# A decoder trunk's last product of values, written as pairs of matmuls of 64 contraction rows

## Chip, cores and metric

The kernel runs on one core of one Trainium2 chip. The metric is the device time of one execution in microseconds (us), the median of several runs. The profile is of one execution; its times count from the first instruction it recorded.

## The reference

Two layers over 256 tokens of width 2048, all in float32. Layer 0 is a Mamba-2 mixer. After it, one product makes the keys and values that the second layer's attention shares. Cut to what matters here:

```python
x = _layer_norm(alpha * x + (1 + gate) * y, ln_g[0], ln_b[0])   # end of layer 0
k, v = jnp.split(x @ kv_w, 2, axis=-1)     # each (256, 3 groups x 8 heads x 128)
...
h = x * (1.0 + scale) + shift              # layer 1 works on h
q, z = jnp.split(h @ b_in_w[0], [3072], axis=-1)
# three head groups of windowed attention over k and v, merged, gated by silu(z)
y = o @ b_out_w[0]
```

## The kernel before

Float32 accuracy is made of three products in the one-pass float32 type F32R: every operand is split into a high part (a rounded copy) and a low part (the rest), and high x high, high x low and low x high are summed in PSUM. Weights stream from HBM in pieces of 128 x 1024: SyncE loads one into `raw` (L118), ScalarE copies it to `whi` (L126), VectorE subtracts for `wlo` (L127).

Contraction runs over 2048 = 16 blocks of 128 rows, `kt`. The activations after layer 0 lie with channels on partitions, in `xhi` and `xlo`: per `kt` a tile of 128 channels x 256 tokens (in the profile they are called `act`).

The values are six products of 512 columns, each by `tm_chunk` (L226): for each of 8 pieces, 2 blocks `kt`, 2 token blocks `b` of 128 and 3 terms, with 128 x 128 activations as the stationary operand and 128 x 512 weights as the moving one: 96 matmuls, on L217, L218 and L219. The two sums, of 128 tokens x 512 columns each, fill one PSUM bank each (`acc`, of the pool `mm` with four banks). `values_out` (L905) then copies each bank to `vt` on ScalarE (L907). The first two products are computed ahead in one loop (L936 to L940), then come the keys (`cm_join`), then the other four products of values (L945).

After them the activations are scaled and shifted in place for layer 1 (L950 to L954), which needs each block `kt` read by all key and value products first. Then `queries` starts (matmuls of L176 and L178), whose products go to other banks of `mm`.

The order on each engine is not that of the source. `arrange` (L1637) takes all recorded instructions with what each depends on, and plans them with a list scheduler. Each instruction has a price (`price`, L1147): for a matmul, how long it holds the engine and how long until its result is there. After eight rounds of planning forward and backward, random changes of the keys are tried, up to 260 rounds in all, and the plan with the earliest end is kept. Matmuls into the same bank keep the order in which they were written; others may be placed in any order that their operands allow. The plan fixes each engine's program; PE runs that program.

Of the kernel before, what the change touches and what calls it, by code (L numbers as in the profile page):

```python
# [11 lines left out]
F32 = mybir.dt.float32  # L12
F32R = mybir.dt.float32r
I32 = mybir.dt.int32
AF = mybir.ActivationFunctionType
ALU = mybir.AluOpType
AX = mybir.AxisListType
PSUM = bass.MemoryType.PSUM
DRAM = bass.MemoryType.DRAM

P = 128
L = 256
D = 2048
KT = D // P
# [47 lines left out]
def trunk(ctx, tc, xT, x, ada0, par, cst, bias, lnrow, ada, wdt, win, wsub, wout, wkv, wk, wbin, wbout, out):  # L72
    nc = tc.nc
    del PINS[:]
    V, S, T = nc.vector, nc.scalar, nc.tensor
# [131 lines left out]
    def tm_piece(src, q, ps, ahi, alo, k0=0, k1=KT, raw=None, n=1):  # L207

        tm_mults(q, split(load_piece(src[q]) if raw is None else raw, n=n), ps, ahi, alo, k0, k1, range(2))
# [13 lines left out]
    def tm_pair():  # L223
        return [mm.tile([P, 512], F32, name="acc") for _ in range(2)]

    def tm_chunk(src, ahi, alo, nk=KT, rate=(0, 1), k0=0, pre=None, keep=()):  # L226

        ps = tm_pair()
        n = nk // 2 - len(keep)
        for q in range(k0 // 2, n):  # L230
            if pre:
                pre(q)
            tm_piece(src, q, ps, ahi, alo, k0, nk)
            background(*rate)
        held = [(q, split(load_piece(src[q]), into=into)) for q, into in zip(range(n, nk // 2), keep)]
        for b in range(2):
            for q, w in held:
                tm_mults(q, w, ps, ahi, alo, k0, nk, (b,))
        return ps
# [29 lines left out]
    def shift(i, kt):  # L269
        return mod[i][:, kt, 0:1]  # L270
# [69 lines left out]
    def drain():  # L340
        while jobs:
            jobs.pop(0)()
# [8 lines left out]
    with ExitStack() as cA:  # L351
# [14 lines left out]
        with ExitStack() as cS:  # L366
# [38 lines left out]
            def product(kind, g, pre=None):  # L405
# [4 lines left out]
                if kind == "z":  # L410
                    ps = tm_chunk(src, hh_, hl_, rate=R, k0=k0, pre=pre)
                    if g not in sz:
# [7 lines left out]
                for w in range(2):  # L420
                    ps = cm_wide(wsub[2 * WSUB.index((kind, g)) + w], hp, hhi, rate=R, k0=k0)
                    for n in range(2):
# [13 lines left out]
            with ExitStack() as c0:  # L436
# [70 lines left out]
                rest = flat[1][:, :512].rearrange("p (j n) -> p j n", j=2)  # L507
# [105 lines left out]
                f, half, low, dots = noted["first"], noted["half"], noted["low"], noted[("dot", 1)]  # L613
# [10 lines left out]
                high, hhis = noted["high"], noted["hhi"]  # L624
# [7 lines left out]
            px = pe = cS.enter_context(tc.tile_pool(name="px", bufs=2, reuse_waits="tile"))  # L632
            R = (1, 5)

# [203 lines left out]
        for n in range(4):  # L838
            ps = tm_chunk(wout[n], lambda kt: yhi[kt // 16][:, kt % 16, :], lambda kt: ylo[kt // 4][:, kt % 4, :],
                          nk=2 * KT, rate=(1, 3) if n else (0, 1), pre=None if n else y_ahead,  # L840
                          keep=[[pa.tile([P, 1024], F32R, name=f"y{2 * i + j}") for j in range(2)] for i in range(HELD)] if n == 3 else ())
# [13 lines left out]
        xp, xhi, xlo = high_low()  # L855
# [41 lines left out]

    with ExitStack() as cL:
        pl = cL.enter_context(tc.tile_pool(name="pl", bufs=3, reuse_waits="tile"))
        R = (2, 5)  # L900
        blocks = [(wk[6 * hq + 2 * g + w], kk[hq][:, g, 2 * w:2 * w + 2, :])
                  for hq in range(2) for g in range(NG) for w in range(2)]
        values = [(wkv[2 * g + hq], vt[hq][:, g]) for hq in range(2) for g in range(NG)]

        def values_out(ps, dst):  # L905
            for b in range(2):
                S.activation(dst[:, b, :], ps[b], AF.Copy)  # L907

        def open_block(b):

            if b:
                open_tiles(b, pl, "xtmp")
            for ps in pss:
                ps.append(mm.tile([P, 512], F32, name="acc"))
            for q in range(NOPEN // 2):
                if b == 0:
                    ws.append([split(load_piece(src[q])) for src, _ in values[:2]])
                for ps, (hi, lo) in zip(pss, ws[q]):
                    for k in range(4):
                        low, k = k // 2, k % 2  # L920
                        h_, l_ = (t[:, 2 * q + k, b * P:b * P + P] for t in (xhi, xlo))
                        if low:
                            T.matmul(ps[b], l_, hi[:, k, :], start=False, stop=False)
                            continue
                        T.matmul(ps[b], h_, hi[:, k, :], start=q == k == 0, stop=False)
                        T.matmul(ps[b], h_, lo[:, k, :], start=False, stop=False)

        pss, ws = [[], []], []
        for b in range(2):
            open_block(b)  # L930
        for c0_ in range(P * NOPEN, D, 512):
            for b in range(2):
                normal(b, c0_, c0_ + 512, b == 0)
        for q in range(NOPEN // 2, KT // 2):
            for i in range(NOPEN if q == NOPEN // 2 else 2 * q + 4, min(2 * q + 6, KT)):
                x_tiles(i, pl, "xtmp")  # L936
            for ps, (src, _) in zip(pss, values):
                tm_piece(src, q, ps, hx, lx)
        for ps, (_, dst) in zip(pss, values):
            values_out(ps, dst)  # L940
        queue(pl, cols1[16:])
        jobs.append(lambda: gate_out(1))
        for src, dst in blocks:
            cm_join(src, dst, rate=R)
        for src, dst in values[2:]:  # L945
            values_out(tm_chunk(src, hx, lx, rate=R), dst)
        drain()

        ada_bias(1, slice(0, KT), slice(0, 2))
        for kt in range(KT):  # L950
            t = pl.tile([P, L], F32, name="htmp")
            S.activation(t, xhi[:, kt, :].bitcast(F32), AF.Identity, bias=shift(1, kt), scale=scale(1, kt))
            V.scalar_tensor_tensor(t, xlo[:, kt, :].bitcast(F32), scale(1, kt), t, op0=ALU.mult, op1=ALU.add)
            split_act(xhi[:, kt, :], xlo[:, kt, :], t)  # L954

        for n in range(4):
            cs_ = slice(512 * n, 512 * n + 512)
            lnr = [pl.tile([P, 512], F32, name=f"lnr{i}", bufs=2) for i in range(2)]
            for i in range(2):
                bcast(lnr[i], lnrow, i * D + 512 * n)  # L960
            for b in range(2):
                V.tensor_tensor(u[b][:, cs_], u[b][:, cs_], lnr[0], op=ALU.mult)
                V.tensor_tensor(u[b][:, cs_], u[b][:, cs_], lnr[1], op=ALU.add)
# [6 lines left out]
    dmat, amask = bs[:, CD:CD + NKEY], bs[:, CA:CA + NKEY]  # L970
    R = (0, 1)

# [82 lines left out]
    for n in range(2):  # L1055
        ps = tm_chunk(wbout[n], *og, nk=H)
# [18 lines left out]
    ps = [tm_pair() for _ in range(2)]  # L1075
# [15 lines left out]
    for i, w in enumerate((slice(0, 256), slice(256, 512))):  # L1091
        c = slice(1536 + w.start, 1536 + w.stop)
        half = (mm.tile([P, 512], F32, name="acc") if i else ps[1][1])[:, :w.stop - w.start]
        for q in range(4):
            hi, lo = held[4 + q]
# [6 lines left out]
    for po_, c in chunks[-1:] + chunks[:-1]:  # L1102
        k, c = c.start // 512, slice(c.start % 512, c.start % 512 + c.stop - c.start)
# [13 lines left out]
    r, mean = ln_scale((1,), st8, False)  # L1117
# [29 lines left out]
def price(x, e):  # L1147

    outs, ins = _aps(x.outs), _aps(x.ins)
    o = outs[0]  # L1150
    if e == "SP":
        return 0.36, 3.0 if str(o.bass_ap.tensor.space) == "DRAM" and hasattr(o.bass_ap.tensor, "tag") else 0.0, None, _n(o) * list(o.ap)[0][1] * 4
    if e == "PE":
        n = _n(ins[0])
        if "float32r" in str(ins[0].dtype):
            return (n / 2400 + 0.0133 if n < 512 else 0.2268), 0.177 + n / 2400, None, 0
        if x.is_transpose:
            return 0.109, 0.273, None, 0
        if list(ins[0].ap)[0][1] == 1:
            return 1.3, 1.5, None, 0  # L1160
        c = max(0.1105, n * 2 / 2400 + 0.0025)
        return 2 * c, c + 0.165 + n * 2 / 2400, None, 0
    n = max(_n(a) for a in ins + [o])
    ps = any(str(a.bass_ap.tensor.space) == "PSUM" for a in ins + [o])
    ptr = sum(_n(a) == 1 for a in ins[1:]) if n > 2 else 0
    if e == "Activation":
        f = str(x.func).split(".")[1]
        d = (0.165 + n / 1190 if ps else 0.19 + n / 1175) + 0.085 * ptr
        return d - 0.095, d, {"Silu": 1, "Exp": 2, "Sqrt": 3}.get(f), 0
    if e == "DVE":  # L1170
        k = type(x).__name__
        if k == "InstReciprocal" and n > 8:
            d = 0.15 + n / 160
        elif k == "InstTensorScalarPtr" and not x.is_scalar_tensor_tensor and not ps:
            d = 0.15 + n / 1850 + 0.05 * (n > 64) + 0.05 * ptr
        else:
            d = 0.152 + n / 960 + 0.057 * ptr
        return d - 0.083 + 0.08 * (len(outs) > 1), d + 0.08 * (len(outs) > 1), None, 0
    return 0.2 + n / 400, 0.2 + n / 370, None, 0
# [572 lines left out]
```

## Time and profile before

| | |
|---|---|
| median of 3 runs | 1241.44 us (1239.98 to 1241.45) |
| the profiled execution: span from first to last instruction | 1238.4 us |
| median above the span | 3.0 us |
| TensorE (PE) busy | 1227.6 us, 99% |
| VectorE (DVE) busy | 1035.9 us, 84% |
| ScalarE (ACT) busy | 703.1 us, 57% |
| HBM traffic | 269 GB/s over the span |

The page has no time of its own for the profiled execution besides the span, so the 3.0 us stand for what lies around it. Busy times are unions of the instructions' durations. PE's matmuls overlap in the array: each lasts longer than the time after which the next one starts, so the spacing of starts is the rate and the duration is not. "PEld" are the loads of the stationary operand. A row of a timeline gives start, duration, engine, line, operation, output and inputs, then the part of the array that the weights fill ("128*16" is 128 rows and 16 columns) and the shape of the moving operand.

### The profile page before, as it was taken

To read this page: it belongs to the slowest core of one execution; us is meant where nothing else is said; L and a number is where in the kernel's file an instruction comes from. 1 tells how busy PE (TensorE), PEld (TensorE's weight loads), DVE (VectorE), ACT (ScalarE), POOL (GpSimd) and SP (SyncE) were. 2 spreads that over 40 slices of the span, in tenths; PEclk is the share of its full clock that TensorE was granted. 3 is DMA by queue.
4 is the path that set the end of the run, shared out by engine and by line. 5 is a ranking of instruction groups with operands and counts; after the bars stand their busy time and mean duration, and the time that the engine had idled before them with its cause. 6 is when DMAs were issued, how large, how long until landed. Compare 5 with 4: busy or idle time off the path is not lost.

```text
span 1238.4 us, 18082 instructions
## 1 busy us (share of the span) xinstructions
PE 1227.6 (99%) x6712; PEld 1058.1 (85%) x6712; DVE 1035.9 (84%) x1481; ACT 703.1 (57%) x1054; POOL 0.2 (0%) x4
## 2 busy tenths in 40 slices
PE   8999999999999999999999999999999999999998
PEld 8889888888888888888888888888888888888886
DVE  6999998989999999978888699998865746757677
ACT  4655466768948589864335455444446644444561
POOL 0000000000000000000000000000000000000000
PEclk9999999999999999999999999999999999999999
DMA  9999977656696855748998669999985563551671
GB/s 368 422 422 421 422 271 241 223 189 234 263 339 224 318 182 190 245 154 294 384 386 308 233 221 369 412 377 378 353 308 187 200 192 103 168 182 64 203 285 68
DMA packets 81743, 334.47 MB, mean 270 GB/s; under 512 B 9108, under 2 KB 9844, under 8 KB 69496
## 3 DMA queue, kind: packets, MB, share of 16 engines
q1 hardware_dynamic: 81656, 333.33, 73.8%
q8 instruction: 52, 0.85, 0.3%
q14 instruction: 35, 0.29, 0.1%
HBM read 331.11 MB, written 2.18 MB: 269 GB/s over the span
## 4 chain that ended last, share of the span: by engine, by line
PE 86%; DMA 11%; DVE 2%; ACT 1%; issue 0%; SPq 0%; ACTq 0%
PE acc L176 27%; PE acc L178 14%; PE acc L217 12%; PE acc L218 12%; PE acc L219 12%; DMA raw<-in_win 8%; DMA araw<-in_ada 2%; PE py L729 2%; PE aux L993 1%; PE aux L699 1%; PE po L1017 1%; PE po L1006 1%; PE aux L994 1%; PE aux L721 1%; DMA y<-in_ada 1%; PE aux L783 0%
## 5 line engine op out<-in xcount | busy, mean ns | idle before, releaser
L126 ACT ACTIVATE whi<-raw 128x1024 fp32r<-128x1024 f32 (+1 forms) x393 | 409.7, 1049 | 342.2 <-PE acc L176 131.6
L127 DVE TENSOR_TENSOR wlo<-raw,whi 128x1024 fp32r<-128x1024 f32 (+1 forms) x393 | 471.2, 1211 | 119.2 <-ACT whi L126 113.3
L176 PE MATMUL acc<-act,whi 128*128 128x512 f32 x1456 | 376.8, 395 | 0.0
L176 PEld LDWEIGHTS acc<-act,whi 128*128 128x128 f32 x1456 | 262.5, 188 | 45.7
L218 PE MATMUL acc<-wlo,act 128*128 128x512 f32 x672 | 257.0, 393 | 0.2 <-DVE wlo L127 0.2
L217 PE MATMUL acc<-whi,act 128*128 128x512 f32 x672 | 249.4, 395 | 1.3 <-ACT whi L126 0.7
L299 DVE SCALAR_TENSOR_TENSOR araw<-araw,cb__72 128x2048 f32<-128x2048 f32 x92 | 210.3, 2285 | 7.0 <-DMA araw<-in_ada 6.7
L178 PE MATMUL acc<-act,wlo 128*128 128x256 f32 x1456 | 212.1, 284 | 0.0
L178 PEld LDWEIGHTS acc<-act,wlo 128*128 128x128 f32 x1456 | 200.4, 190 | 13.5 <-issue 0.5
L219 PE MATMUL acc<-whi,act 128*128 128x512 f32 x432 | 163.0, 392 | 0.0
L218 PEld LDWEIGHTS acc<-wlo,act 128*128 128x128 f32 x672 | 126.0, 188 | 27.1 <-DVE wlo L127 1.1
L217 PEld LDWEIGHTS acc<-whi,act 128*128 128x128 f32 x672 | 125.3, 188 | 27.8 <-ACT whi L126 1.2
L219 PEld LDWEIGHTS acc<-whi,act 128*128 128x128 f32 x432 | 81.1, 188 | 16.7 <-issue 0.7
L219 PE MATMUL acc<-whi,ylo 128*128 128x512 f32 x240 | 89.8, 392 | 0.0
L219 PEld LDWEIGHTS acc<-whi,ylo 128*128 128x128 f32 x240 | 45.0, 188 | 9.3 <-DVE ylo L789 0.2
L164 PE MATMUL acc<-act,whi 128*128 128x256 f32 x208 | 51.6, 284 | 0.8 <-ACT whi L126 0.4
L165 PE MATMUL acc<-act,wlo 128*128 128x256 f32 x208 | 51.9, 284 | 0.0
L162 PE MATMUL acc<-act,whi 128*128 128x256 f32 x208 | 42.0, 284 | 0.0
L164 PEld LDWEIGHTS acc<-act,whi 128*128 128x128 f32 x208 | 38.0, 191 | 2.4 <-ACT whi L126 0.6
L687 ACT ACTIVATE seg<-cbc,cumT 128x128 f32<-128x128 f32 x128 | 39.8, 389 | 0.0
L165 PEld LDWEIGHTS acc<-act,wlo 128*128 128x128 f32 x208 | 38.1, 191 | 0.8
L384 DVE SCALAR_TENSOR_TENSOR cacc<-ct,prm,cacc 128x255 f32<-128x255 f32 (+2 forms) x84 | 36.2, 477 | 1.0 <-ACT cacc L381 0.9
(269 smaller groups left out, 1147.1 us busy)
## 6 DMA issues: line engine op xcount, KB each, us to landing
araw<-in_ada SPq DMA_DIRECT2D x92, 1024.0 KB, 7.3
raw<-in_win SPq DMA_DIRECT2D x86, 512.0 KB, 9.8
raw<-in_wsub SPq DMA_DIRECT2D x70, 512.0 KB, 4.4
raw<-in_wout SPq DMA_DIRECT2D x64, 512.0 KB, 5.2
raw<-in_wbin SPq DMA_DIRECT2D x64, 512.0 KB, 3.4
raw<-in_wkv SPq DMA_DIRECT2D x48, 512.0 KB, 4.7
raw<-in_wk SPq DMA_DIRECT2D x48, 512.0 KB, 6.7
cbc<-cumd SPq DMA_DIRECT2D x16, 512.0 KB, 5.0
```

Source lines behind the costliest of these rows:

```text
L126: a = S.activation(hi[:, c_], raw[:, c_], AF.Copy)
L127: m = V.tensor_tensor(lo[:, c_], raw[:, c_], hi[:, c_].bitcast(F32), op=ALU.subtract)
L162: T.matmul(o, hi[:, k, c_], alo[:, kt, :], start=False, stop=kt == k1 - 1, skip_group_check=True)
L164: note("product", T.matmul(o, hi[:, k, c_], ahi[:, kt, :], start=kt == k0 and n % 2 == 0, stop=False, skip_group_check=True))
L165: T.matmul(o, lo[:, k, c_], ahi[:, kt, :], start=False, stop=False, skip_group_check=True)
L176: T.matmul(ps[n], hi[:, k, c_], both[:, kt], start=first, stop=False, skip_group_check=True)
L178: T.matmul(ps[n][:, 0, :], lo[:, k, c_], high[:, kt, :], start=first, stop=False, skip_group_check=True)
L217: begin = T.matmul(ps[b], h_, hi[:, k, :], start=kt == k0, stop=False)
L218: T.matmul(ps[b], h_, lo[:, k, :], start=False, stop=False)
L219: end = T.matmul(ps[b], l_, hi[:, k, :], start=False, stop=kt == k1 - 1)
L299: V.scalar_tensor_tensor(raw, raw, 1.0, cb_, op0=ALU.mult, op1=ALU.mult, accum_out=to)
L687: m = S.activation(seg[:, hh, b, :], cbc[:, hh, b, :], AF.Relu, bias=cumT[:, b, h0 + hh:h0 + hh + 1], scale=-1.0)
```

## The change

The sixth and last product of values is no longer made by `tm_chunk`. A new `rows_chunk` writes each of its 96 matmuls as two: one with the channels in partitions 0 to 63, called `low` in the source, and one with those in partitions 64 to 127, called `high`. (By partition number, `low` is the lower half, and so it is called below.) Each works on 64 contraction rows and all 512 columns. The two sum into banks of their own, `low` in two banks of `mm` (`acc` in the profile) and `high` in two banks of a new pool `rest`. At the end ScalarE copies each `high` bank to `vt` and VectorE adds the `low` bank to it.

The price of an F32R matmul with fewer than 128 contraction rows is new as well: it holds the engine for 0.1134, where a full one of 512 columns has 0.2268, and its result is there after 0.39, as for the full one. The whole program is planned anew with it, and the order of instructions differs in all stages.

```diff
+        rest = cL.enter_context(tc.tile_pool(name="rest", bufs=2, space=PSUM))
...
+        def rows_chunk(src, dst, rate):
+            low, high = tm_pair(), [rest.tile([P, 512], F32, name="rest") for _ in range(2)]
+            for q in range(KT // 2):
+                hi, lo = split(load_piece(src[q]))
+                for k in range(2):
+                    kt = 2 * q + k
+                    for b in range(2):
+                        h_, l_ = (t[:, kt, b * P:b * P + P] for t in (xhi, xlo))
+                        for i, (x_, w_) in enumerate(((h_, hi), (h_, lo), (l_, hi))):
+                            for ps, r in ((low, slice(0, 64)), (high, slice(64, P))):
+                                T.matmul(ps[b], x_[r], w_[r, k, :], start=kt == i == 0, stop=kt == KT - 1 and i == 2)
+                background(*rate)
+            for b in range(2):
+                S.activation(dst[:, b, :], high[b], AF.Copy)
+                V.tensor_tensor(dst[:, b, :], low[b], dst[:, b, :], op=ALU.add)
...
-        for src, dst in values[2:]:
+        for src, dst in values[2:5]:
             values_out(tm_chunk(src, hx, lx, rate=R), dst)
+        for src, dst in values[5:]:
+            rows_chunk(src, dst, R)
...
         if "float32r" in str(ins[0].dtype):
+            if list(ins[0].ap)[0][1] < P:
+                return 0.1134, 0.39, None, 0
             return (n / 2400 + 0.0133 if n < 512 else 0.2268), 0.177 + n / 2400, None, 0
```

In the changed kernel the new matmuls are line 921.

## The prediction, as it was put on record

> **What bounds the kernel now.** I read the page first: its head, the busy times and the 40 slices.
>
> ```profile
> span 1238.4 us, 18082 instructions
> PE 1227.6 (99%) x6712; PEld 1058.1 (85%) x6712; DVE 1035.9 (84%) x1481; ACT 703.1 (57%) x1054; POOL 0.2 (0%) x4
> PEclk9999999999999999999999999999999999999999
> PE 86%; DMA 11%; DVE 2%; ACT 1%; issue 0%; SPq 0%; ACTq 0%
> ```
>
> TensorE (PE) is busy all the time, at full granted clock, and makes up 86% of the chain that ended last. The table of windows shows whether this holds at the place of the change.
>
> ```profile
> 900.00:1000.00 100.00, 100.00 (x485) 84.39 (x485) 65.36 (x84) 55.29 (x78) 0.00 (x0) 1.00 0.66 224
> 946.00:972.00 26.00, 26.00 (x122) 21.62 (x122) 22.52 (x39) 22.68 (x41) 0.00 (x0) 1.00 0.57 196
> ```
>
> The columns are the window, its length, then busy time (and instructions) of PE, PEld, DVE, ACT and POOL, the clock, the DMA share and GB/s. The window from 946 to 972 us is that of the last product of values: the timeline of ScalarE has the copies of the product before it at 946.25 and 949.34, and its own at its end.
>
> ```profile
> 946.25 0.60 ACT L907 ACTIVATE vt<-acc 128x512 f32<-128x512 f32 x1 [0.53 <-PE acc L219]
> ...
> 970.49 0.57 ACT L907 ACTIVATE vt<-acc 128x512 f32<-128x512 f32 x1
> ...
> 972.52 0.59 ACT L907 ACTIVATE vt<-acc 128x512 f32<-128x512 f32 x1
> ```
>
> PE has no idle time there, so a microsecond of PE's stream put in or taken out in this stage moves the end by a microsecond, as long as what feeds it keeps up. How long one matmul holds PE is read from starts, not from its duration, which includes the way through the array. Timeline of PE:
>
> ```profile
> 947.19 0.39 PE L217 MATMUL acc<-whi,act 128*128 128x512 f32 x1
> ...
> 952.86 0.39 PE L217 MATMUL acc<-whi,act 128*128 128x512 f32 x1
> ```
>
> Between these two rows' starts lie 25 matmuls of 512 columns: 5.67/25 = 0.2268 us each. The product has 16 blocks of contraction rows, 2 blocks of tokens and 3 terms, so 96 matmuls, 96 x 0.2268 = 21.8 us.
>
> **What a half matmul costs.** The change makes 192 matmuls of these 96, each with 64 contraction rows and still 512 moving columns. No trace row has one of 64 rows, so I bound it. These groups say what a duration follows:
>
> ```profile
> L176 PE MATMUL acc<-act,whi 128*128 128x512 f32 x1456 | 376.8, 395 | 0.0
> L178 PE MATMUL acc<-act,wlo 128*128 128x256 f32 x1456 | 212.1, 284 | 0.0
> L783 PE MATMUL aux<-cc,y 128*128 128x128 f32 x64 | 10.2, 272 | 0.0
> ...
> L323 PE MATMUL aux<-cc,mod x2: 270/270/270, 446.2 to 956.5; 128*16 128x128 f32 x2
> ```
>
> With half the moving columns the mean falls from 395 to 284 ns. Filling less of the array does not help: L323, which loads 16 of the 128 columns (its row gives least, median and greatest), takes 270 ns, and L783, which loads all, 272. So a matmul's own time follows its moving columns, which the change keeps, and a half matmul alone should hold its half for 0.2268 us. The two halves can share a slot of 0.2268 us (0.1134 each, which the planner's new price says), or each takes its own (0.2268 each). Those are the two ends: 21.8 us for the product as before, or 192 x 0.2268 = 43.5 us, 21.8 more.
>
> Which of them holds depends on the order, and here the change does something that its text does not show. The source writes the lower and the upper half of a pair next to each other, but the planner places each matmul for itself. On PE, in the middle of the product, where acc_8905 and acc_8906 are the two token blocks' banks, the kernel before has:
>
> ```order
> L217 MATMUL acc_8905<-whi_8928,act0_6760 128x512
> L218 MATMUL acc_8905<-wlo_8929,act0_6760 128x512
> L219 MATMUL acc_8905<-whi_8928,act0_6760 128x512
> L217 MATMUL acc_8906<-whi_8928,act0_6760 128x512
> L218 MATMUL acc_8906<-wlo_8929,act0_6760 128x512
> L219 MATMUL acc_8906<-whi_8928,act0_6760 128x512
> ```
>
> The changed one has there, with acc_8908 and acc_8909 for the lower half and rest_8910 and rest_8911 for the upper:
>
> ```order
> L921 MATMUL acc_8908<-whi_8945,act0_6760 128x512
> L921 MATMUL acc_8908<-wlo_8946,act0_6760 128x512
> L921 MATMUL acc_8908<-whi_8945,act0_6760 128x512 x2
> L921 MATMUL acc_8908<-wlo_8946,act0_6760 128x512
> L921 MATMUL acc_8908<-whi_8945,act0_6760 128x512
> L921 MATMUL acc_8908<-whi_8975,act0_6760 128x512
> L921 MATMUL rest_8910<-whi_8945,act0_6760 128x512
> L921 MATMUL rest_8910<-wlo_8946,act0_6760 128x512
> L921 MATMUL rest_8910<-whi_8945,act0_6760 128x512
> L921 MATMUL acc_8909<-whi_8945,act0_6760 128x512
> ```
>
> Seven of the lower half stand in a row, then three of the upper, then the lower again: the pairs are torn apart. Two matmuls for the same half cannot share a slot. At the end of the product the kernel before has:
>
> ```order
> L217 MATMUL acc_8906<-whi_9042,act1_6761 128x512
> L218 MATMUL acc_8906<-wlo_9043,act1_6761 128x512
> L219 MATMUL acc_8906<-whi_9042,act1_6761 128x512
> L176 MATMUL acc_9183<-act0_6760,whi_9186 128x512
> L218 MATMUL acc_8905<-wlo_9043,act1_6761 128x512
> L219 MATMUL acc_8905<-whi_9042,act1_6761 128x512
> ```
>
> And the changed one:
>
> ```order
> L921 MATMUL acc_8908<-whi_9131,act1_6761 128x512 x2
> L921 MATMUL acc_8908<-wlo_9132,act1_6761 128x512
> L921 MATMUL acc_8908<-whi_9131,act1_6761 128x512
> L921 MATMUL acc_8909<-whi_9131,act1_6761 128x512 x2
> L921 MATMUL acc_8909<-wlo_9132,act1_6761 128x512
> L921 MATMUL acc_8909<-whi_9131,act1_6761 128x512
> L921 MATMUL rest_8911<-whi_9131,act1_6761 128x512
> L921 MATMUL rest_8911<-wlo_9132,act1_6761 128x512
> L921 MATMUL rest_8911<-whi_9131,act1_6761 128x512
> L176 MATMUL acc_9286<-act0_6760,whi_9290 128x512 x4
> ```
>
> Eight of the lower half, three of the upper, then the queries' first full matmuls. Does PE take later ones early? The trace of the kernel before, at that end:
>
> ```profile
> 967.96 0.39 PE L217 MATMUL acc<-whi,act 128*128 128x512 f32 x1
> 968.18 0.39 PE L218 MATMUL acc<-wlo,act 128*128 128x512 f32 x1
> 968.41 0.39 PE L219 MATMUL acc<-whi,act 128*128 128x512 f32 x1
> 968.64 0.39 PE L176 MATMUL acc<-act,whi 128*128 128x512 f32 x1
> 968.86 0.39 PE L218 MATMUL acc<-wlo,act 128*128 128x512 f32 x1
> ```
>
> It is the program's order to the last matmul, though L176 and L218 go to different banks. [...]
>
> So I count with three rules: order is kept; a half matmul holds its half for 0.2268 us; it may start with the one ahead of it if that is of the other half and shares its slot with no other. Over the whole product the 192 stand in 59 unbroken runs of one half, up to 11 long, with 54 direct changes of half (9 full matmuls, 8 of them of the product before, stand between the others). Going through the list, 45 times two share a slot, which leaves 192 - 45 = 147 slots, where 96 were before: 51 x 0.2268 = 11.6 us more.
>
> **The other terms.** Switching between full and half matmuls happens 10 times. The nearest row is the transpose that loads 16 columns amid full matmuls:
>
> ```profile
> 517.28 1.04 PE L783 MATMUL aux<-cc,y 128*128 128x128 f32 x8
> ...
> 956.26 0.39 PE L219 MATMUL acc<-whi,act 128*128 128x512 f32 x1
> 956.48 0.27 PE L323 MATMUL aux<-cc,mod 128*16 128x128 f32 x1
> 956.51 0.48 PE L217 MATMUL acc<-whi,act 128*128 128x512 f32 x1
> 956.82 0.39 PE L218 MATMUL acc<-wlo,act 128*128 128x512 f32 x1
> ```
>
> From 956.26 to 956.82 are 0.56 us; two full matmuls take 0.454 of it and a transpose (1.04 - 0.27)/7 = 0.11, as in L783. Nothing is left for a drain; I take 0. [...] This row shows none for columns. A drain here could be no more than the way through the array, 0.39 - 0.2268 = 0.16 us, so 1.6 us for ten; that is the upper end. A slot could also end 0.0125 us sooner where two share it, or last 0.013 longer if two weight loads need it; the chain in order of time has both prices:
>
> ```profile
> 976.62 1.68 PE acc L178 x14
> 978.31 3.64 PE acc L176 x16
> ```
>
> A matmul of 256 columns, with its own weight load, takes 0.120 us and one of 512 takes 0.2275: twice 0.120 less 0.2275 is 0.0125 of fixed cost, and two loads fit in 0.240. Over 45 shared slots either is 0.6 us; I take 0. The evacuation gains two additions on VectorE, each like
>
> ```profile
> L730 DVE TENSOR_TENSOR y<-py,y 128x512 f32<-128x512 f32 x16 | 10.9, 683 | 0.1
> ```
>
> so 1.4 us, in a window where DVE is busy 22.5 of 26 us and which grows by 11.6; the values are wanted only by the second half of the heads, much later: 0. Without that cover it would be 1.4. ScalarE still makes two copies. Loads and splits are as many as before, ahead of a slower PE: 0. The scale and shift of the activations (L952), written in place, follow the last reader block by block as before: 0. The planner's search gave a new order for all of the kernel; PE idles 1238.4 - 1227.6 = 10.8 us in all, most of it at the start and the end, and no row says that the new order waits more or less: 0, with 2 us either way.
>
> The sum is +11.6 us on the profiled execution, 1238.4 to 1250.0 of span; the median of the runs shown, 1241.44, lies 3.0 above the span, so 1253.0. About 0.2% (2.5 us) is what a measurement can tell here.
>
> **Rivals.** First, PE keeps two streams, so that pairs overlap however they stand: all 192 fit in 96 slots, for 1241.4, or 1240.2 if the fixed 0.0125 is hidden 96 times. It decides if one half can run ahead of the other by a run of up to 11 matmuls. This is the way to no loss at all. [...] The trace speaks against it with its kept order of starts. I give it 0.12. Second, no overlap at all: 192 slots, 21.8 us more, 1263.2, and up to 1264.8 with the drains. No row shows two matmuls at one time, which is for it, and nothing in this kernel has been shown to share the array; 0.24. Third, the new order elsewhere happens to save or avoid PE's idle time beside the first rival; this alone makes it faster, by 3 us or more: 0.04. The forecast has 0.60.
>
> **How the numbers follow.** The forecast's own range is 1253.0 less 0.6 and 2, plus 0.6, 1.6 and 2: 1250 to 1257. The second rival's is 1261 to 1267. A range from 1249 to 1266 takes in the forecast and nearly all of the second rival, 0.8 together; the first and third lie below it. Faster: 0.04. Same: 0.10, of the first rival; its remaining 0.02 goes to slower, with the forecast and the second rival, 0.86.
>
> **What would show it.** In the changed profile, the product's window should be 11.6 us longer and PE still busy throughout; starts in a run of one half 0.227 us apart; at a change of half, two starts close together; at the switches nothing. Starts 0.227 apart at changes of half too would show the second rival; starts 0.113 apart inside runs the first. The argument is wrong if runs of one half go faster than 0.2268 per matmul, or if the stage grows and the end does not move.

## The result, and the profile after

The changed kernel takes 1247.45 us (median; 1246.21 to 1247.82), the kernel before, in four runs, 1241.0: a ratio of 1.0052, 95% interval 1.0037 to 1.0066. It is slower, as forecast, but by 6.45 us and not by 11.6. The forecast of 1253.0 and the range from 1249 both miss it.

Lines of the page of the changed kernel that answer to those of before:

```profile
span 1246.0 us, 18268 instructions
PE 1233.8 (99%) x6808; PEld 1063.3 (85%) x6808; DVE 1038.9 (83%) x1483; ACT 707.4 (57%) x1056; POOL 0.2 (0%) x4
```

PE is as full as before: 96 matmuls and 96 weight loads more. The profiled execution itself took 1247.82 us, 1.8 above its span. (The spans of the two profiles differ by 7.6 us; each is of one execution, so the medians count for the difference.) The window of the product and the groups of its matmuls:

```profile
946.00:977.00 31.00, 31.00 (x212) 25.49 (x211) 20.16 (x33) 21.24 (x36) 0.00 (x0) 1.00 0.45 144
```

```profile
L921 PE MATMUL rest<-whi,act 64*128 64x512 f32 x64 | 21.1, 400 | 0.0
L921 PE MATMUL acc<-wlo,act 64*128 64x512 f32 x32 | 12.3, 399 | 0.0
```

A half matmul lasts as long as a full one (400 against 395 ns on average), as predicted from the moving columns. The surprise is in the starts. First, the timeline of PE in the first full stretch of halves:

```profile
951.43 0.49 PE L921 MATMUL rest<-whi,act 64*128 64x512 f32 x1
951.44 0.49 PE L921 MATMUL acc<-whi,act 64*128 64x512 f32 x1
951.77 0.39 PE L921 MATMUL rest<-whi,act 64*128 64x512 f32 x1
951.77 0.39 PE L921 MATMUL acc<-wlo,act 64*128 64x512 f32 x1
952.00 0.39 PE L921 MATMUL acc<-whi,act 64*128 64x512 f32 x1
952.00 0.39 PE L921 MATMUL rest<-whi,act 64*128 64x512 f32 x1
952.23 0.39 PE L921 MATMUL acc<-wlo,act 64*128 64x512 f32 x1
952.24 0.39 PE L921 MATMUL rest<-wlo,act 64*128 64x512 f32 x1
```

In PE's program the same matmuls stand next to each other in this order (numbered here from 1; `rest` is the upper half):

```
1 rest whi
2 acc whi     3 acc wlo     4 acc whi     5 acc wlo
6 rest whi
7 acc whi
8 rest whi    9 rest wlo
```

The upper half's second matmul, number 6, starts at 951.77, together with number 3 and ahead of 4 and 5. So PE does not keep the program's order between the halves: each half runs its own in order, 0.227 us apart and never less than 0.224, and here a matmul started while up to three earlier ones of the other half had not. Matching all 192 starts to the program, each half's in its order (the names of the weights, `whi` or `wlo`, then agree for every one), the number of earlier matmuls still to come is 0, 1, 2 or 3 and never more: 18 times it is three.

The same timeline where the lower half stands eleven times in a row:

```profile
956.60 0.39 PE L921 MATMUL rest<-whi,act 64*128 64x512 f32 x1
956.68 0.39 PE L921 MATMUL acc<-wlo,act 64*128 64x512 f32 x1
956.90 0.84 PE L921 MATMUL acc<-whi,act 64*128 64x512 f32 x3
...
958.26 0.39 PE L921 MATMUL acc<-whi,act 64*128 64x512 f32 x1
958.27 0.49 PE L921 MATMUL rest<-whi,act 64*128 64x512 f32 x1
958.49 0.39 PE L921 MATMUL acc<-whi,act 64*128 64x512 f32 x1
```

From 956.83, 0.227 us after its matmul of 956.60, until 958.27 the upper half has nothing to do: its next matmul stands behind the run, and starts when three of the run are still to come. Here a run costs time. And at the first change from full matmuls to halves and back:

```profile
947.16 0.39 PE L218 MATMUL acc<-wlo,act 128*128 128x512 f32 x1
947.48 0.49 PE L921 MATMUL rest<-whi,act 64*128 64x512 f32 x1
947.49 0.49 PE L921 MATMUL acc<-whi,act 64*128 64x512 f32 x1
947.91 0.50 PE L219 MATMUL acc<-whi,act 128*128 128x512 f32 x1
948.24 0.40 PE L217 MATMUL acc<-whi,act 128*128 128x512 f32 x1
948.48 0.39 PE L219 MATMUL acc<-whi,act 128*128 128x512 f32 x1
```

From 947.16 to 948.48 are 1.32 us for three full matmuls and a pair, which at 0.2268 each is 0.91: one visit to the halves costs 0.41. The pair itself starts within 0.01 us.

The stretch of the product, with the 8 full matmuls and the transpose inside it, runs from 947.48 to 976.10 (the last start is at 975.87), 28.6 us. The same work in the kernel before, 104 x 0.2268 + 0.11, is 23.7. So 4.9 of the 6.45 us are lost in the product. To split them I worked the list of starts through by three rules: a half's matmuls 0.2268 apart, at most three overtaken, and the step prices just seen (0.095 more into the halves, 0.194 out, 0.11 for a first step after an idle time). The rules give 28.5 us, and the starts deviate from the measured ones by 0.09 us on average. Without changing prices it is 26.2, with an unlimited reach besides 24.6. So, roughly, taking the terms off one after the other: 0.9 us for halves that stand alone between full matmuls, 1.6 for runs beyond the reach, 2.3 for changing and restarting.

### The profile page after: what moved, and what is told of

Same layout as the page of the kernel before. It is cut to its first block, busy times and chain, and to the rows that moved or that the text cites. A ratio compares the mean times of both kernels' runs of the same rounds, so it can differ in the third digit from the quotient of the medians.

```text
span 1246.0 us, 18268 instructions
## 1 busy us (share of the span) xinstructions
PE 1233.8 (99%) x6808; PEld 1063.3 (85%) x6808; DVE 1038.9 (83%) x1483; ACT 707.4 (57%) x1056; POOL 0.2 (0%) x4
## 4 chain that ended last, share of the span: by engine, by line
PE 81%; DMA 11%; DVE 4%; ACT 3%; issue 1%; SPq 0%; DVEq 0%; ACTq 0%
PE acc L176 26%; PE acc L178 13%; PE acc L217 10%; PE acc L218 10%; PE acc L219 10%; DMA raw<-in_win 9%; DMA araw<-in_ada 2%; PE py L729 2%; DVE wlo L127 1%; ACT whi L126 1%; PE acc L921 1%; PE rest L921 1%; DVE araw L299 1%; PE aux L1013 1%; PE po L1037 1%
## 5 line engine op out<-in xcount | busy, mean ns | idle before, releaser
L218 PE MATMUL acc<-wlo,act 128*128 128x512 f32 x640 | 245.1, 394 | 0.4 <-DVE wlo L127 0.4
L217 PE MATMUL acc<-whi,act 128*128 128x512 f32 x640 | 237.9, 394 | 1.5 <-ACT whi L126 0.6
L219 PE MATMUL acc<-whi,act 128*128 128x512 f32 x400 | 150.0, 392 | 0.0
L217 PEld LDWEIGHTS acc<-whi,act 128*128 128x128 f32 x640 | 119.8, 188 | 26.4 <-ACT whi L126 0.8
L218 PEld LDWEIGHTS acc<-wlo,act 128*128 128x128 f32 x640 | 120.0, 188 | 25.8 <-DVE wlo L127 1.0
L219 PEld LDWEIGHTS acc<-whi,act 128*128 128x128 f32 x400 | 75.1, 188 | 16.0 <-issue 1.1
```

Of the source, the lines that this page charges most:

```text
L217: begin = T.matmul(ps[b], h_, hi[:, k, :], start=kt == k0, stop=False)
L219: end = T.matmul(ps[b], l_, hi[:, k, :], start=False, stop=kt == k1 - 1)
```

## The experiments

Theory W is this reading: two streams with a reach of three, and a price for changing between full and half matmuls. Rival I is the prediction's (order kept, only neighbours overlap), rival H says that a pair simply costs more, whatever its order. To hold everything else fixed, the first five kernels start from the plan of the kernel before, and the first four keep it instruction for instruction: the planner sees each pair as one full matmul, and the second half and the two additions are put in afterwards. ScalarE copies the lower bank there and VectorE adds the upper one. Times of the kernel before are 1240.84 us in each comparison below.

**Pairs kept together.** The edit, on the plan's way into the program:

```diff
+            if x.name in pair:
+                h, q = pair[x.name]
...
+                out.append((e, x))
+                held.append(h)
+                if len(held) == RUN:
+                    put()
```

`x` is a lower half, at the place of its full matmul, `h` its upper half, and `put` writes the held ones; `RUN` is 1 here, 3 and 12 in the next two.

> The order of the kernel before is kept, instruction for instruction; only each matmul of the last product of values becomes two of 64 rows, the second right behind the first, and the two additions are put in behind the copies. Theory W (the halves are two streams, of which one may start a matmul ahead of at most three earlier ones that have not started; a visit from full matmuls to halves and back costs 0.4 us; the rest of the loss came from the new order elsewhere): all pairs overlap, six visits cost 2.6 us, so 1243.6 us. Rival H (a pair costs more whatever its order, 0.278 us for 0.227, since the product took 4.9 us more): 1245.9. Rival I (order kept, only neighbours overlap): the same pairs overlap here, 1241.0 to 1243.6.

Measured: 1243.27 us, ratio 1.0017 (1.0008 to 1.0026), so 2.4 more than before. The timeline of PE shows a steady stretch, and then what a transpose that loads 16 columns (L327) does in it:

```profile
957.83 0.39 PE L930 MATMUL rest<-whi,act 64*128 64x512 f32 x1
957.83 0.39 PE L929 MATMUL acc<-whi,act 64*128 64x512 f32 x1
958.06 0.39 PE L930 MATMUL rest<-wlo,act 64*128 64x512 f32 x1
958.06 0.39 PE L929 MATMUL acc<-wlo,act 64*128 64x512 f32 x1
958.28 0.39 PE L930 MATMUL rest<-whi,act 64*128 64x512 f32 x1
958.29 0.39 PE L929 MATMUL acc<-whi,act 64*128 64x512 f32 x1
958.60 0.28 PE L327 MATMUL aux<-cc,mod 128*16 128x128 f32 x1
958.82 0.50 PE L929 MATMUL acc<-whi,act 64*128 64x512 f32 x1
...
959.15 0.39 PE L929 MATMUL acc<-wlo,act 64*128 64x512 f32 x1
```

The halves of a pair start together, and the pairs 0.23 us apart: in a stretch without changes a pair costs what one full matmul did, so rival H is out. From 958.28 to 959.15, around the transpose, 0.87 us go by where 0.2268 + 0.11 + 0.2268 = 0.56 are due.

**Runs of three.** The same with `RUN = 3`. A run ends early where a full matmul or the next piece of weights comes, so runs are of one to three, here and, up to twelve, in the next kernel.

> As the paired kernel, but three of one half stand before the three of the other. Theory W: runs of three are within its reach of three, so all overlap and the time is that of the paired kernel, 1243.6 us, product 2.6 us longer than before. Rival I: a run shares only one slot with the next, 128 slots for 96, 7.3 us more than the paired kernel: 1250.9. Rival H: 1245.9.

Measured: 1243.15 us, ratio 1.0016 (1.0008 to 1.0025), the same as with adjacent pairs. Rival I expected 1250.9 here and is out: PE overtakes.

**Runs of twelve.** `RUN = 12`.

> As the paired kernel, but up to twelve of one half stand before those of the other (as many as one piece of weights has between other matmuls). Theory W: runs beyond eight leave one half waiting; worked through the order with a reach of three, the product takes 7.6 us more than before, 5.0 more than paired: 1248.6 us. Rival I: 159 slots, 14.3 us more than paired: 1257.9. Rival H: no change against paired, 1245.9.

Measured: 1248.09 us, ratio 1.0057 (1.0045 to 1.0070): 4.8 us above the paired kernel, where W had 5.0 and the rivals 14.3 and none. Its timeline, at the end of a run of the upper half:

```profile
959.29 0.39 PE L929 MATMUL acc<-whi,act 64*128 64x512 f32 x1
959.38 0.61 PE L930 MATMUL rest<-whi,act 64*128 64x512 f32 x2
959.83 0.39 PE L930 MATMUL rest<-wlo,act 64*128 64x512 f32 x1
960.06 0.39 PE L930 MATMUL rest<-whi,act 64*128 64x512 f32 x1
960.38 0.28 PE L327 MATMUL aux<-cc,mod 128*16 128x128 f32 x1
960.59 0.49 PE L929 MATMUL acc<-whi,act 64*128 64x512 f32 x1
960.92 0.39 PE L929 MATMUL acc<-wlo,act 64*128 64x512 f32 x1
961.16 0.39 PE L929 MATMUL acc<-whi,act 64*128 64x512 f32 x1
961.16 0.49 PE L930 MATMUL rest<-whi,act 64*128 64x512 f32 x1
```

The upper half runs alone at the end of its run, and the lower alone after the transpose, until the upper's first comes within reach. In this kernel, too, no matmul overtakes more than three: in the trace from 955.80 to 962.55 us five overtake exactly three. By the same rules its stretch takes 31.4 us with a reach of three, 33.4 with two and 30.1 with four; in the trace it takes 31.6.

**Many changes.** Only the third term in halves, so that pairs and full matmuls alternate:

```diff
-                            if i not in (0, 1, 2):
+                            if i not in (2,):
                                 T.matmul(low[b], x_, w_[:, k, :], start=kt == i == 0, stop=ends)
```

> As the paired kernel, but only the third term of each product is made in halves, so that 32 pairs stand among full matmuls and the array changes between full and halves some 30 times each way. Theory W: each visit costs 0.4 to 0.5 us, 13.7 us in all: 1254.7 us. If changing costs nothing, as the prediction took from the transpose: 1241.0. Rival H: 32 pairs at 0.05 us, 1242.6.

Measured: 1252.31 us, ratio 1.0089 (1.0075 to 1.0103): 11.5 more than before, 0.41 us for each of 28 visits. Changing is not free, though it costs less than W had it: 1254.7 lies above the interval, which ends at 1253.6. One visit in its timeline:

```profile
955.04 0.39 PE L927 MATMUL acc<-wlo,act 128*128 128x512 f32 x1
955.36 0.49 PE L929 MATMUL acc<-whi,act 64*128 64x512 f32 x1
955.37 0.49 PE L930 MATMUL rest<-whi,act 64*128 64x512 f32 x1
955.79 0.50 PE L927 MATMUL acc<-whi,act 128*128 128x512 f32 x1
956.13 0.40 PE L927 MATMUL acc<-wlo,act 128*128 128x512 f32 x1
956.37 0.40 PE L927 MATMUL acc<-whi,act 128*128 128x512 f32 x1
```

The steps are 0.32, 0.43, 0.34 and then 0.24. From 955.04 to 956.37 that is 1.33 us for 0.91 due, 0.42 for the visit. The expected 13.7 us had counted the longer first step of a half, 0.11, in visits of one pair too, which have no second step.

**Gathered.** The paired kernel, with the full matmuls that stood among the halves put ahead of or behind them:

```diff
+    head = [i for i in full if i < pe[len(pe) // 4] and i not in tp]
+    tail = [i for i in full if i not in head and i not in tp]
...
+    want = [out[i] for i in head + rest_ + tail]
```

Here `tp` is the transpose, and `rest_` the halves with it.

> As the paired kernel, but the full matmuls that stood among the halves are put ahead of all halves or behind them, save one transpose, so that TensorE changes to halves and back twice instead of six times. Theory W: each visit costs about 0.4 us, so 0.8 us more than before, 1241.7 us, and 1.6 to 1.8 us less than the paired kernel. If the paired kernel's 2.4 us are a price of the halves themselves (0.025 us a pair): 1243.3, as the paired kernel.

Measured: 1241.21 us, ratio 1.0002 (0.9993 to 1.0011): no difference from before, and 2.1 us less than the paired kernel, where W had 1.6 to 1.8 less, and a price of the halves themselves would leave no difference. The two visits are still there in its timeline:

```profile
946.15 0.39 PE L223 MATMUL acc<-whi,act 128*128 128x512 f32 x1
946.47 0.49 PE L929 MATMUL acc<-whi,act 64*128 64x512 f32 x1
...
968.62 0.39 PE L930 MATMUL rest<-whi,act 64*128 64x512 f32 x1
968.94 1.66 PE L180 MATMUL acc<-act,whi 128*128 128x512 f32 x6
```

From the last full matmul ahead of the halves to the first behind them are 22.79 us, for 97 x 0.2268 + 0.11 = 22.11 due. Those 0.7 us are less than the interval of the times can tell, which goes from 0.9 below before to 1.4 above. So with pairs together and the changes down to two visits, the halves cost no more than the times can tell from nothing, and bring nothing.

**The new order, with full matmuls.** The program is planned as the changed kernel, then written with one full matmul at the place of each pair's later half, with the two copies of the kernel before and without the two additions:

```diff
+                            if PLAN[0] is not None:
+                                T.matmul(low[b], x_, w_[:, k, :], start=kt == i == 0, stop=kt == KT - 1 and i == 2)
+                                continue
```

> The order of the changed kernel in everything else, but each pair of halves made one full matmul again, at the place of the later half, with the two copies of the kernel before and without the two additions. Theory W: the product loses its 4.9 us, and what is left above the kernel before is the new order elsewhere: 1247.4 - 4.9 = 1242.5 us, 1.6 above. If the halves cost it all: 1241.0. If the prediction's own view held, that the new order costs nothing and that waits do not differ: 1241.0 too.

Measured: 1242.08 us, ratio 1.0012 (1.0003 to 1.0020): 1.2 us above before, where W had 1.6, and 5.4 below the changed kernel. So the halves account for about 5 us and the order elsewhere for about 1.

**New orders alone.** The kernel before, with another seed in the planner:

```diff
-    key, best, near = [float(v.i) for v in P[0]], None, random.Random(0)
+    key, best, near = [float(v.i) for v in P[0]], None, random.Random(1)
```

> The kernel before, with another seed for the planner's random changes of its keys (1 for 0), so that the order differs everywhere and the work nowhere. It measures what a new order alone does: if plans of equal cost to the planner differ by less than 2 us on the chip, 1239 to 1243 us; if the order of the kernel before is an unusually good one, 1242 to 1244.

> As the run with seed 1, with seed 2: 1239 to 1243 us if new orders scatter about the old, 1242 to 1244 if the old one is unusually good.

Measured: 1240.90 us, ratio 1.0001 (0.9992 to 1.0011), and 1241.54, ratio 1.0008 (1.0000 to 1.0017). These two new orders differ from the old by 0.1 and 0.7 us; the 1.2 of the changed kernel's order lies a little beyond them, and by its interval may be anything from 0.4 to 2.5. It is there before the last product starts: up to 946 us the kernel with that order and full matmuls runs 5089 matmuls where the kernel before has 5095, and six of 512 columns are 1.4 us. Which waits add up to it was not traced further.

## Why the prediction was wrong

- **What bounds the kernel.** Right: PE is full throughout (99% busy, before and after), the product's stretch grew by 4.9 us and the end by 6.45. That it came out slower is only in part for my reason: of the 6.45 us some 2.5 come from halves without a partner within reach, 2.3 from changes and restarts, and 1.2 from the new order elsewhere, and the last two I had at nothing.
- **A half matmul holds its half for 0.2268 us, and two share a slot.** Right: steps of 0.227 within a half, pairs that start within 0.01 us (paired kernel, all 21 from 957.83 to 962.80).
- **Order is kept (the step that failed).** I counted 147 slots on the rule that a half matmul may start only with its direct neighbour, 11.6 us. The evidence for it was a stretch of full matmuls in program order, which could not show it: every matmul there uses both halves, so the row says nothing of two matmuls in different halves. With halves PE started one ahead of up to three others here, 18 times of exactly three. Runs beyond that, and halves alone between full matmuls, cost 2.5 us in place of 11.6. The runs of three show it by themselves: 1243.15 us where my rule gives 1250.9.
- **Changing between full and half matmuls at 0 (mis-sized).** It costs 0.41 us a visit, so 0.2 us a change, where my upper end had 0.16, the 0.39 less 0.2268 of a matmul: 2.0 us for the five visits here, above my 1.6 for ten changes, and 2.3 with the restarts. The transpose of 16 columns, from which I took 0, still uses all 128 rows and says nothing of a change in rows; the transpose amid pairs, which does change them, costs 0.3. No run shows a drain, on which that upper end was counted, or what else PE does in that time; what they show is the 0.41 us a visit.
- **The new order elsewhere at 0.** Measured 1.2 us, inside the 2 us I allowed.
- **The first rival** had the mechanism, two streams, and the point from which it decides: the reach against the length of the runs. I asked only whether the reach covers runs of eleven. It is three, so the truth lies between the rival and the forecast, and a range that leaves out the cases between two rivals misses it.
- **Evacuation, loads and in-place scaling at 0.** Nothing in the profile contradicts it: the gathered kernel has the additions and the halves and takes the time of before, within its interval.

## What to carry to other kernels

A planner that prices half matmuls at half a slot must also know that here the two halves were two streams with a reach of three: keep the halves of a pair within three matmuls of each other, and halves together with halves, since each visit from full matmuls and back cost 0.4 us here. The contraction was already full here, and splitting it into two halves had nothing to give; the best order only got back to the time of before (1241.21 against 1240.84 us). And evidence for a rule of order has to come from instructions that could have broken it.

## What the runs showed of the hardware

- A half matmul started ahead of up to three earlier ones of the other half of the rows, never of more: exactly three 18 times in the changed kernel, and five times in that with runs of twelve from 955.80 to 962.55 us. Why three was not tried.
- Two half matmuls started together 0.23 us after the pair before them (paired kernel), with two weight loads in that time: in the changed kernel those of the pair of 952.00 start at 951.77 and 951.78.
- After a change from full matmuls a half's second matmul came 0.335 us after the first, not 0.227 (951.44 to 951.77 above), and so it did after a half had to wait (958.27 above, the next at 958.61), 0.11 us more. The weight load of the first started with the matmul itself (951.44), that of the second 0.11 us later and 0.23 ahead of its matmul (951.54 for 951.77), as in the steady stretch (951.77 for 952.00). Whether the loads make the 0.11 us no experiment took apart.
- The first half matmuls after such a change or wait, 19 of the 192 in the changed kernel, lasted 0.49 to 0.50 us by the profile, not 0.39, and in all 19 the weight load started within 0.002 us of the matmul.
